# A hybrid pooling and linear-attention block in fp32: the norm row spread by a product, P4 second in the first pair, values of a head pair asked for among the gates

## The chip, the cores and the metric

One NeuronCore of a Trainium2 chip runs the whole block. The metric is the device time of one execution in microseconds (us); smaller is better. The core has a matrix engine (TensorE, PE in the profile; PEld is its loading of stationary operands), a vector engine (VectorE, DVE), a scalar engine (ScalarE, ACT), GpSimd (POOL) and SyncE (SP), which here only issues DMA transfers. Matrix products accumulate in PSUM, which the kernel uses as eight banks of 128 x 512 fp32; everything else lies in the on-chip memory or in DRAM. A bank can be written again once the engine that reads it is through.

## What is computed

The reference, cut to what matters (L is 16 meta tokens and 1024 tokens, D is 1024, the inner width of the MLP 4096, four heads of key width 64 and value width 128, chunks of 64):

```python
def rmsnorm(x, g):
    return x * lax.rsqrt(jnp.mean(x * x, axis=-1, keepdims=True) + EPS) * g

def hybrid_mixer(u, ...):
    z = jnp.einsum('bld,dn->bln', u, w_in)
    a, q, k, v, r, lr, ga, gb = jnp.split(z, IN_SPLITS, axis=-1)
    p = multiscale_pool(a)                      # trailing means over 2, 4, 8, 16 tokens, minus the token
    ...
    y_a = jnp.einsum('blc,cd->bld', p, w_pool_out)
    log_a = jax.nn.log_sigmoid(lr @ w_gate_up + b_gate) / GLA_TAU
    o = gla_chunked(q, k, v, log_a)             # chunked gated linear attention with a carried state
    o = rmsnorm(o, gla_norm) * jax.nn.silu(r)
    y_b = jnp.einsum('blc,cd->bld', o, w_gla_out)
    m = jax.nn.sigmoid(ga) * y_a + jax.nn.sigmoid(gb) * y_b
    return jnp.einsum('bld,de->ble', m, w_out)

def reference(x, meta_tokens, norm_mix, ...):
    h = jnp.concatenate([meta, x], axis=1)
    h = h + hybrid_mixer(rmsnorm(h, norm_mix[l]), ...)
    h = h + squared_relu_mlp(rmsnorm(h, norm_ffn[l]), w_ff1[l], w_ff2[l])
    return rmsnorm(h, norm_final)[:, N_META:]
```

## The kernel before

**Products.** Every large product is computed as three products of a reduced fp32 type: an operand is split into a high half (copied with rounding by ACT) and a low half (the remainder, subtracted by DVE), and `mm3` (L256) issues high by high, low by high and high by low (L260 to L262). Weights arrive from DRAM as `raw` tiles, and their split is a step on ACT (L609, L75, L341) and one on DVE (L610, L76, L342). Tile names in the profile follow this: `th` and `tl` are the halves of the activations, `w1h` and `w1l` those of a weight, `fs` and `s` sums of weight blocks that POOL or DVE make.

**Opening (`start`, L390 on).** `load(t)` brings a tile of 128 tokens of x, `layer_norm` (L227) normalizes it: ACT squares and sums, DVE makes the inverse root and multiplies by it and by `gB`, the weights of the norm repeated on all 128 partitions (L234, tile `us`). `gB` is filled by one transfer (L414). `transposed` (L238) turns a tile on PE into banks `ms` and `sc` (L246), from which ACT and DVE make `th` (L202) and `tl` (L203). `v_tile` (L350) makes the values of a tile and of the first two heads, with 16 more columns, `lr`, which DVE copies to `lrtok` (L364); the values go to DRAM as `v_dram`. `ask_vw` and `load_vw` (L331, L336) load and split the weights of the values (`vw`) and `lrraw`, those of the lr columns. `warm` (L409) multiplies a blank tile, so that PE has something to do: six products of 512 columns before the first tile, more small ones later.

**Eleven pairs of projections (`pairs_of_projections`).** Each pair of 128-column projections of q, r and the two gates, on both halves of the tokens, is computed by seven products P1 to P7 of sums of blocks instead of eight products of blocks. P1 and P2 of a pair share one bank of kind `sc`; ACT copies P1 away as `u2p` (L720) before P2 is added. P5 and P3 share a bank of kind `z`, of which there are two; P4, P6 and P7 take one of two banks `y`. DVE adds P6 to `u2p` (L724), P7 to that, giving `u3p` (L726), and then makes two of the four results: `c` from P5 and `u3p` (L728), and `c` from P4 and `u3p` (L732). `pairs_order` (L633) sets the order: P1, P2, P5 of the first pair, then seven products at a time, from pair i and the one before. `ahead(..., 3)` has the weights of each product split three products earlier; the first one's are made in `first_pair`, before the stage. Beside these products ACT, DVE and POOL work on the chunks of the attention: keys, decays, and the q values, which come back from `q_dram` as `gi` (L852) and are copied by ACT to `f` and `n` (L865).

**Attention and gates.** `gla_open` (L917) asks for the attention's inputs (`gi`), for gates (`ask`, L957: from `ga_dram`, later from `gb_dram` with the sums in `ma_dram`; 16 tiles of L965 in a ring) and for the values (`v`, L937). `across` (L1040 on) transposes the keys (L1055), copies them to `kt` (ACT, L1056), and multiplies them with the values (L1061). Where it yields a number, other products (output products of the pooling mixer and of the attention, bank `mm`) are put on PE in between, for that many us times `PACE` (L1127). A gate is opened by ACT (an exponential, L970), and the output products are read with it by DVE (L1025, L1026).

**What sets the order.** PE runs its instructions in the order in which the program is written, and so the kernel's generators (`ahead`, the yields, `pour`) decide it. For ACT, DVE, POOL and SP a scheduler orders the instructions when the program is built; each of these runs its row strictly in order. All transfers of the program go through SP's row.

**After it.** The MLP: FF1 by seven products as above (rows `b_sc`, `b_z`, `b_y` until 926 us), then FF2 (`b_o`), whose first product waits for DVE (L1361), and the last norm.

Of the kernel before, what the change touches and what calls it, by code (L numbers as in the profile page):

```python
# [11 lines left out]
ALU = mybir.AluOpType  # L12
# [18 lines left out]
MP = 264  # L31
PACE, LEVEL, OPENING, STRETCH = 1.3, 1.6, 6.0, 1.9

# [70 lines left out]
def kernel(  # L104
# [286 lines left out]
    def start():  # L391
# [19 lines left out]
        load(0)  # L411
        warm(6)
        nc.sync.dma_start(ident, ident_in)
        nc.sync.dma_start(gB, bcast(norm_mix))  # L414
# [145 lines left out]
    k_(1)  # L560
    step(one, lambda: S["last_difference"]())

# [70 lines left out]
    def pairs_order(n_pairs):  # L633
        yield from (("P1", 0), ("P2", 0), ("P5", 0))
        for i in range(1, n_pairs + 1):
            for p in ("P6", "P1", "P7", "P5", "P4", "P2", "P3"):
                n = i if p in ("P1", "P5", "P2") else i - 1
                if n < n_pairs:
                    yield p, n

    def sums_weights(order, n_pairs, load, eng):
# [5 lines left out]
        for p, i in order(n_pairs):  # L647
# [3 lines left out]
            else:  # L651
                a21, a22 = (w1raw[i, 1][:, k : k + 4] for k in (0, 4))
                s = quad(S["fs"][:, i % 2] if p != "P7" else S["s3"])
                if p == "P5":
# [33 lines left out]
    def pairs_of_projections():  # L688
# [18 lines left out]
        for n, (p, i, (ah, al)) in enumerate(ahead(pair_weights(), 3)):  # L707
# [3 lines left out]
            elif p in ("P5", "P3"):  # L711
                b = zb[i] = bank("z") if p == "P5" else zb[i]
            else:
                b = bank("y")
# [10 lines left out]
            elif p == "P7":  # L725
# [3 lines left out]
                put(d + 1, 1, c, c)  # L729
            elif p == "P4":  # L730
                c = nxt("c")
# [15 lines left out]
            if total - n <= 6:  # L747
                assert chain is None
                if total - n > 2:
                    pooled_part(n - total + 6)  # L750
            if total - n == 3:
                raw.back()
                W1.shift = 1
                enqueue(rest)
                W1.top_up(1)
            yield
# [160 lines left out]
    def gla_open():  # L917
# [11 lines left out]
        lend("c", "t1", "o")  # L929
        wanted[:] = [("a", d, h) for d in range(8) for h in range(2)] + [("b", d, 0) for d in range(8)]  # L930
        for p in range(2):
            fetch(p, 0)
        ask()
        for half in range(2):
            for p in range(2):
                t = slice(4 * half, 4 * half + 4)
                nc.sync.dma_start(S["v"][:, p, t], v_dram[p, t].rearrange("t p c -> p t c"))  # L937
        banks(keep=1, mm=3, m2=1, ms=1)
# [15 lines left out]

    def ask():

        while wanted:  # L957
            kind, d, h = wanted[0]
# [82 lines left out]
    def across(p, half):  # L1041
# [14 lines left out]
        act.activation(kt, b, ACT.Copy)  # L1056
        yield 1.4
        kv = wide2().rearrange("p u (j c) -> p u j c", j=4)
# [477 lines left out]
```

## Time and profile before

| | |
|---|---|
| three runs | 1250.29, 1251.13, 1251.39 us; median 1251.13 |
| the profiled execution, own time | 1249.28 us |
| its span | 1247.4 us |
| mean granted clock of PE | 0.996 |
| PE busy | 1213.6 us, 97% of the span |
| weight loads (PEld) | 997.3 us, 80% (beside PE) |
| DVE busy | 866.0 us, 69% |
| ACT busy | 635.3 us, 51% |
| POOL busy | 72.2 us, 6% |
| HBM | 153 GB/s over the span |

The span is the stretch between the first and the last instruction of the profiled execution; its own time is that of the whole launch. PE's row of the page is at 9 tenths or more in all but the first and the last of 40 slices, so that what is idle on PE lies in short waits. They are to be found in the list of waits, and each of them then in a window of single rows: start and length in us, engine, line, operation, written tile `<-` read tiles, shape, and in brackets the idle time before it with the tile for which the engine waited.

### The profile page before, as it was taken

What the parts mean: (1) busy time and instruction counts of PE and PEld (TensorE: products, weight loads), DVE (VectorE), ACT (ScalarE), POOL (GpSimd) and SP (SyncE); (2) the same over time, 40 slices, a digit from 0 to 9 for tenths busy, and PEclk for the clock granted to TensorE, in tenths of its full rate; (3) what the DMA queues carried; (4) which work ended last, traced back from release to release, by engine and by line L of the source; (5) the groups of instructions that cost most, each with busy time, mean ns of one, the idle gap of its engine ahead of it and who ended that gap; (6) DMA issues with size and microseconds to landing.
All of it is one profiled execution on the core that took longest, in us unless ns stands there. A gap on an engine that the chain in (4) does not pass through costs nothing.

```text
span 1247.4 us, 18416 instructions
## 1 busy us (share of the span) xinstructions
PE 1213.6 (97%) x6807; PEld 997.3 (80%) x6807; DVE 866.0 (69%) x1421; ACT 635.3 (51%) x1119; POOL 72.2 (6%) x95
## 2 busy tenths in 40 slices
PE   8999999999999999999999999999999999999997
PEld 6999877777777778788778888888878788888776
DVE  5635548796877478844897676676664887887686
ACT  7623456767576434523655454554554444445454
POOL 0000042322321000000000000000000000000000
PEclk9999999999999999999999999999999999999999
DMA  8212342434347976941245444444579763333532
GB/s 259 81 39 85 94 127 76 136 97 141 80 134 229 327 264 200 311 138 51 101 125 161 145 157 150 157 152 144 168 241 368 274 214 102 102 93 93 169 91 86
DMA packets 153401, 192.23 MB, mean 154 GB/s; under 512 B 12096, under 2 KB 89168, under 8 KB 153312
## 3 DMA queue, kind: packets, MB, share of 16 engines
q1 hardware_dynamic: 153312, 191.06, 47.6%
q8 instruction: 53, 0.87, 0.3%
q14 instruction: 36, 0.29, 0.1%
HBM read 129.14 MB, written 61.88 MB: 153 GB/s over the span
## 4 chain that ended last, share of the span: by engine, by line
PE 76%; DVE 9%; DMA 8%; ACT 4%; issue 3%; SPq 1%; POOL 0%; DVEq 0%; ACTq 0%; POOLq 0%
PE b_o L261 7%; PE b_o L262 7%; PE b_o L260 7%; PE b_mm L262 6%; PE b_mm L260 6%; PE b_mm L261 6%; PE b_y L260 5%; PE b_y L261 5%; PE b_y L262 5%; PE b_sc L260 3%; PE b_sc L261 3%; PE b_z L260 3%; PE b_sc L262 3%; PE b_z L261 3%; PE b_z L262 3%
## 5 line engine op out<-in xcount | busy, mean ns | idle before, releaser
L609 ACT ACTIVATE w1h<-raw 128x512 fp32r<-128x512 f32 x106 | 66.0, 624 | 61.0 <-PE b_sc L261 19.5
L260 PE MATMUL b_sc<-th,w1h 128*128 128x512 f32 x216 | 86.4, 400 | 2.5 <-ACT u2p L720 1.8
L261 PE MATMUL b_sc<-tl,w1h 128*128 128x512 f32 x216 | 85.5, 396 | 0.0
L260 PE MATMUL b_z<-th,w1h 128*128 128x512 f32 x216 | 85.3, 395 | 0.2 <-DVE c L728 0.2
L262 PE MATMUL b_sc<-th,w1l 128*128 128x512 f32 x216 | 85.1, 394 | 0.0
L610 DVE TENSOR_TENSOR w1l<-raw,w1h 128x512 fp32r<-128x512 f32 x106 | 72.5, 684 | 18.0 <-ACT w1h L609 18.0
L261 PE MATMUL b_z<-tl,w1h 128*128 128x512 f32 x216 | 84.2, 390 | 0.4 <-DVE tl L1221 0.4
L262 PE MATMUL b_z<-th,w1l 128*128 128x512 f32 x216 | 84.1, 390 | 0.0
L260 PE MATMUL b_o<-w1h 128*128 128x512 f32 x192 | 75.6, 394 | 2.8 <-DVE h L1361 1.8
L609 ACT ACTIVATE w1h<-fs 128x512 fp32r<-128x512 f32 x81 | 50.9, 629 | 51.7 <-PE b_y L261 29.9
L261 PE MATMUL b_o<-w1l,w1h 128*128 128x512 f32 x192 | 75.6, 393 | 1.4 <-DVE w1l L610 1.4
L262 PE MATMUL b_o<-w1h,w1l 128*128 128x512 f32 x192 | 75.5, 393 | 0.1
L260 PE MATMUL b_mm<-th,w1h 128*128 128x512 f32 (+1 forms) x208 | 72.0, 346 | 0.9 <-DVE c L736 0.9
L610 DVE TENSOR_TENSOR w1l<-fs,w1h 128x512 fp32r<-128x512 f32 x81 | 56.8, 702 | 20.7 <-ACT w1h L609 20.6
L261 PE MATMUL b_mm<-tl,w1h 128*128 128x512 f32 (+1 forms) x208 | 71.1, 342 | 0.0
L262 PE MATMUL b_mm<-th,w1l 128*128 128x512 f32 (+1 forms) x208 | 71.0, 341 | 0.0
L609 ACT ACTIVATE w1h<-bt 128x512 fp32r<-128x512 f32 x45 | 28.3, 630 | 56.8 <-issue 33.0
L1409 DVE TENSOR_TENSOR bt<-w,w 128x512 f32<-128x512 f32 x80 | 54.7, 684 | 2.7 <-DMA w<-in_w_ff_dram 2.7
L260 PEld LDWEIGHTS b_sc<-th,w1h 128*128 128x128 f32 x216 | 40.9, 190 | 13.5 <-ACT u2p L720 2.2
L261 PE MATMUL b_o<-fxl,fxh 128*128 128x512 f32 x128 | 49.9, 390 | 0.7 <-DVE small L219 0.7
L260 PE MATMUL b_mm<-wo,th 128*128 128x512 f32 x128 | 50.4, 394 | 0.0
L262 PE MATMUL b_o<-fxh,fxl 128*128 128x512 f32 x128 | 49.9, 390 | 0.0
(375 smaller groups left out, 3345.7 us busy)
## 6 DMA issues: line engine op xcount, KB each, us to landing
hf_dram<-h SPq DMA_DIRECT2D x112, 256.0 KB, 2.1
raw<-hf_dram SPq DMA_DIRECT2D x112, 256.0 KB, 2.6
w<-in_w_ff_dram SPq DMA_DIRECT2D x64, 256.0 KB, 4.7
raw<-in_w_in_dram SPq DMA_DIRECT2D x22, 512.0 KB, 4.7
raw<-in_w_ff_dram SPq DMA_DIRECT2D x16, 512.0 KB, 4.2
rawx<-in_w_ff_dram SPq DMA_DIRECT2D x16, 512.0 KB, 4.3
rawp<-in_w_in_dram SPq DMA_DIRECT2D x10, 512.0 KB, 4.6
xs<-in_x_dram SPq DMA_DIRECT2D x8, 512.0 KB, 5.5
```

Of the source, the lines that this page charges most:

```text
L260: pe.matmul(ps, ah, bh, start=first and i == 0, stop=False, skip_group_check=more)
L261: pe.matmul(ps, ah, bl, start=False, stop=False, skip_group_check=more)
L262: pe.matmul(ps, al, bh, start=False, stop=last and i == n - 1, skip_group_check=more)
L609: act.activation(hi, a, ACT.Copy)
L610: dve.tensor_tensor(lo, a, f32(hi), ALU.subtract)
L1409: dve.tensor_tensor(bt, w, S["w2"][q[3:]][:, i], ALU.add if q[2] == "+" else ALU.subtract)
```

## The change

The diff without its rows of numbers:

```diff
-PACE, LEVEL, OPENING, STRETCH = 1.3, 1.6, 6.0, 1.9
+PACE, LEVEL, OPENING, STRETCH = 1.3, 1.6, 5.0, 1.9
...
         load(0)
-        warm(6)
+        nc.sync.dma_start(um[:1], norm_mix[None, :])
         nc.sync.dma_start(ident, ident_in)
-        nc.sync.dma_start(gB, bcast(norm_mix))
+        ask_vw(0)
+        nc.sync.dma_start(S["lrraw"], w_in[:, C_LR : C_LR + 16].rearrange("(k p) c -> p k c", p=P))
+        pool.memset(xm[:1, :P], 1.0)
+        warm(2)
+        for c in halves():
+            b = bank("mm")
+            pe.matmul(b, xm[:1, :P], um[:1, c], start=True, stop=True)
+            dve.tensor_copy(gB[:, c], b)
+        warm(2)
         for t in range(8):
...
             if t == 0:
-                nc.sync.dma_start(S["lrraw"], w_in[:, C_LR : C_LR + 16].rearrange("(k p) c -> p k c", p=P))
-                ask_vw(0)
                 load(1)
...
-    step(one, lambda: S["last_difference"]())
+    def after_keys():
+        S["first"] += [next(S["pw"]) for _ in range(2)]
+        S["last_difference"]()
+
+    step(one, after_keys)
...
     def pairs_order(n_pairs):
-        yield from (("P1", 0), ("P2", 0), ("P5", 0))
+        yield from (("P1", 0), ("P4", 0), ("P2", 0), ("P5", 0))
         for i in range(1, n_pairs + 1):
             for p in ("P6", "P1", "P7", "P5", "P4", "P2", "P3"):
                 n = i if p in ("P1", "P5", "P2") else i - 1
-                if n < n_pairs:
+                if n < n_pairs and (p, n) != ("P4", 0):
                     yield p, n
...
+            elif (p, i) == ("P4", 0):
+                b = early = bank("z")
             else:
                 b = bank("y")
...
                 put(d + 1, 1, c, c)
-            elif p == "P4":
+                if i == 0:
+                    c = nxt("c")
+                    dve.tensor_tensor(c, early, u3, ALU.add)
+                    put(d + 1, 0, c, c)
+            elif p == "P4" and i:
...
+        def values(p, half):
+            t = slice(4 * half, 4 * half + 4)
+            nc.sync.dma_start(S["v"][:, p, t], v_dram[p, t].rearrange("t p c -> p t c"))
+
+        ask(2)
         for p in range(2):
             fetch(p, 0)
+            values(p, 0)
         ask()
-        for half in range(2):
-            for p in range(2):
-                t = slice(4 * half, 4 * half + 4)
-                nc.sync.dma_start(S["v"][:, p, t], v_dram[p, t].rearrange("t p c -> p t c"))
+        for p in range(2):
+            values(p, 1)
...
-    def ask():
+    def ask(most=16):
 
-        while wanted:
+        while wanted and S["io_live"] < most:
...
         act.activation(kt, b, ACT.Copy)
-        yield 1.4
+        yield 2.4
         kv = wide2().rearrange("p u (j c) -> p u j c", j=4)
```

Three lines that do nothing else are left out: the loads of W1 before the last three products stand a few lines earlier, and the sum for P4 needs no buffer of its own.

**The opening.** One row of the norm's weights (4 KB) is loaded to `um`; PE multiplies a row of ones with it, once for each half, and DVE copies the two results from PSUM to `gB` (L421 of the changed kernel). The six warming products become two ahead and two behind these. The weights of the values are asked for at the start, `lrraw` behind them.

**The first pair.** P4 is computed second, into a bank of kind `z`, and read (L744 of the changed kernel) after P7, since it needs `u3p`. On DVE's row, before, from the sum with P6 on (`rawp` and `raw` are loaded weights, L610 makes the low half of one):

```order
L724 TENSOR_TENSOR u2p<-b_y,u2p 128x512 [waits PE_49]
L610 TENSOR_TENSOR w1l<-raw_123,w1h 128x512 [waits DMAHW0_49,Activation_49]
L610 TENSOR_TENSOR w1l<-rawp_1639,w1h 128x512 [waits PE_49,Activation_49]
L726 TENSOR_TENSOR u3p<-b_y,u2p 128x512 [waits DVE_49,PE_49]
L610 TENSOR_TENSOR w1l<-fs,w1h 128x512 [waits Activation_49]
L728 TENSOR_TENSOR c<-b_z,u3p 128x512 [waits DMAHW7_49,DMAHW3_49,DVE_49]
L610 TENSOR_TENSOR w1l<-fs,w1h 128x512 [waits PE_49,Activation_49]
L732 TENSOR_TENSOR c<-b_y,u3p 128x512 [waits DMAHW4_49,DMAHW0_49,PE_49]
```

and of the change:

```order
L736 TENSOR_TENSOR u2p<-b_y,u2p 128x512 [waits PE_49]
L620 TENSOR_TENSOR w1l<-rawp_1646,w1h 128x512 [waits Activation_49]
L620 TENSOR_TENSOR w1l<-fs,w1h 128x512 [waits PE_49,Activation_49]
L738 TENSOR_TENSOR u3p<-b_y,u2p 128x512 [waits DVE_49,PE_49]
L620 TENSOR_TENSOR w1l<-fs,w1h 128x512 [waits Activation_49]
L740 TENSOR_TENSOR c<-b_z,u3p 128x512 [waits DMAHW7_49,DMAHW3_49,DVE_49]
L744 TENSOR_TENSOR c<-b_z,u3p 128x512 [waits DMAHW4_49,DMAHW0_49]
```

The reading of P4 moved up behind that of P5, from another bank. On PE's row P5 of the second pair, the first product behind P7, waits for DVE's reading at L744, since the ring of two z banks is full; before, this row waited for the high half on ACT alone. Elsewhere in the stage the rows of ACT, DVE and SP keep their order, apart from the weights of P4, P2 and P5, which are split two products earlier.

**Values among the gates.** SP's row at the opening of the attention (L584 is a store of gates, L965 or L985 the load of one, `v<-v_dram` the values of one head pair and half; four in all), before:

```order
L584 DMA ga_dram<-t_1011 128x512 [waits DMAHW4_49,DVE_49]
L965 DMA c<-ga_dram 128x512 [waits DMAHW5_49,Activation_49]
L937 DMA v<-v_dram 128x4x256 [waits DMAHW6_49,PE_49]
L584 DMA ga_dram<-t_1011 128x512 [waits DMAHW7_49,DVE_49]
L965 DMA c<-ga_dram 128x512 [waits DMAHW0_49,Activation_49]
L584 DMA ga_dram<-t_1011 128x512 [waits DMAHW1_49,DVE_49]
L965 DMA c<-ga_dram 128x512 [waits DMAHW2_49,Activation_49]
L965 DMA t_1011<-ga_dram 128x512 [waits DMAHW4_49,DMAHW3_49]
L965 DMA t_1011<-ga_dram 128x512 [waits DMAHW7_49]
L965 DMA t_1011<-ga_dram 128x512 [waits DMAHW5_49,DMAHW1_49]
L937 DMA v<-v_dram 128x4x256 [waits DMAHW6_49]
```

and of the change:

```order
L594 DMA ga_dram<-t_1014 128x512 [waits DMAHW4_49,DVE_49]
L949 DMA v<-v_dram 128x4x256 [waits DMAHW5_49,PE_49]
L594 DMA ga_dram<-t_1014 128x512 [waits DMAHW6_49,DVE_49]
L985 DMA c<-ga_dram 128x512 [waits DMAHW7_49,Activation_49]
L949 DMA v<-v_dram 128x4x256 [waits DMAHW0_49]
L594 DMA ga_dram<-t_1014 128x512 [waits DMAHW1_49,DVE_49]
L985 DMA c<-ga_dram 128x512 [waits DMAHW2_49,Activation_49]
```

The second head pair's values moved from behind seven loads of gates and the three stores among them to the place behind the second.

**Later rows that moved.** The longer yield after `kt` shifts six products of other work ahead of the state products in one half, and six in the other. Between 470 and 525 us the scheduler also places loads and splits otherwise; on SP's row, around the load of a weight of the attention's output (`in_w_gla_out`), before:

```order
L965 DMA o<-ma_dram 128x512 [waits DMAHW4_49]
L965 DMA t_4838<-gb_dram 128x512 [waits DMAHW5_49,DVE_49]
L965 DMA t_4838<-ma_dram 128x512 [waits DMAHW6_49]
L965 DMA t_4838<-gb_dram 128x512 [waits DMAHW7_49]
L965 DMA t_4838<-ma_dram 128x512 [waits DMAHW0_49]
L99 DMA raw_4852<-in_w_gla_out_dram 128x4x256 [waits DMAHW1_49]
```

and of the change:

```order
L985 DMA o<-ma_dram 128x512 [waits DMAHW3_49]
L99 DMA raw_4855<-in_w_gla_out_dram 128x4x256 [waits DMAHW4_49]
L985 DMA t_4841<-gb_dram 128x512 [waits DMAHW5_49,DVE_49]
L985 DMA t_4841<-ma_dram 128x512 [waits DMAHW6_49]
L985 DMA t_4841<-gb_dram 128x512 [waits DMAHW7_49]
L985 DMA t_4841<-ma_dram 128x512 [waits DMAHW0_49]
```

The weight load moved ahead of four loads of gates and sums, and its low half on DVE moved ahead with it. Outside these places (the opening to 30 us, 150 to 180, 404 to 525) each engine's row is the same as before.

More of the change, by code (lines that the diff above doesn't have):

```diff
@@ L652, in sums_weights @@
                 a21, a22 = (w1raw[i, 1][:, k : k + 4] for k in (0, 4))
-                s = quad(S["fs"][:, i % 2] if p != "P7" else S["s3"])
+                s = None if p == "P4" else quad(S["fs"][:, i % 2] if p != "P7" else S["s3"])
                 if p == "P5":
@@ L748, in pairs_of_projections @@
                 assert chain is None
+                if total - n == 3:
+                    raw.back()
+                    W1.shift = 1
+                    enqueue(rest)
+                    W1.top_up(1)
                 if total - n > 2:
                     pooled_part(n - total + 6)
[L751 to L755, printed above, removed]
             yield
```

## The prediction

> **What bounds the kernel now.** I read the page's head first, then the waits of the matrix engine (PE), then windows around the two longest, and only then single rows.
>
> ```profile
> span 1247.4 us, 18416 instructions
> PE 76%; DVE 9%; DMA 8%; ACT 4%; issue 3%; SPq 1%; POOL 0%; DVEq 0%; ACTq 0%; POOLq 0%
> ```
>
> The first line is the span of the profiled execution, whose own time is 1249.28 us: 1.9 us lie around the span, and it stands 1.85 us under the median of the runs, 1251.13. The second is the chain of work that ended last: three quarters of it are PE. Nothing else is a bound for long, so a change is worth what it adds to or takes from PE's idle time, and what it does to PE's clock.
>
> ```profile
> PE b_sc L260 <- ACT u2p L720: 1.8, 1, 1.8
> PE b_o L260 <- DVE h L1361: 1.8, 1, 1.8
> PE b_m L1061 <- ACT kt L1056: 1.6, 1, 1.6
> PE b_sc L1061 <- DMA v<-v_dram: 1.5, 1, 1.5
> PE b_mm L260 <- ACT th L202: 1.2, 1, 1.2
> PE b_mm L260 <- ACT w1h L75: 1.1, 1, 1.1
> PE b_sc L246 <- DVE lrtok L364: 1.0, 1, 1.0
> PE b_mm L262 <- DVE w1l L76: 0.6, 1, 0.6
> PE b_mm L260 <- DVE t L1025: 0.5, 1, 0.5
> ```
>
> These are PE's waits: who waited, for whom, us in total, times, longest. Each happens once. The change touches all but the second of them (the start of the last stage, far behind every edit).
>
> ```profile
> 154.34:157.75 3.41, 1.60 (x8) 1.00 (x7) 1.16 (x2) 1.11 (x2) 2.78 (x4) 1.00 0.70 185
> 157.75:161.16 3.41, 3.41 (x10) 2.65 (x9) 1.22 (x3) 1.15 (x2) 1.52 (x3) 0.50 0.73 195
> 925.75:929.16 3.41, 1.65 (x7) 0.94 (x7) 3.41 (x7) 1.79 (x4) 0.00 (x0) 1.00 0.92 321
> 929.16:932.57 3.41, 3.41 (x9) 2.62 (x9) 2.11 (x4) 0.44 (x1) 0.00 (x0) 0.50 0.99 324
> 452.68:456.09 3.41, 1.88 (x9) 1.18 (x7) 2.12 (x3) 1.06 (x3) 0.00 (x0) 1.00 0.71 196
> ```
>
> Windows: the stretch, its length, busy time of PE, weight load, DVE, ACT and POOL, then the granted clock. I cut them at multiples of 3.413 us from 7.56, where the clock's changes fall in this trace. Where PE was busy for 1.60 or 1.65 of 3.41 us, the next 3.41 us ran at clock 0.50; with 1.88 it stayed at 1.00. So about 1.71 us of idle inside one such window costs, besides itself, half of the next, 1.7 us. The wait for u2p therefore costs 1.81 + 1.70 = 3.5 us, and that for h as much.
>
> The Trainium skill ("TensorE: Matmul & The Clock Gate", Part 1: The HAM clock gate (the "warmup" mystery)) gives a free-running window of 4096 cycles at 1.2 GHz, 3413 ns, which this trace's changes of clock fit; it names an idle window of about 3.4 us as what halves the clock, and there the trace differs: 1.81 and 1.76 us of idle inside one window sufficed.
>
> **The opening: −1.0 us.**
>
> ```profile
> 1.45 8.44 PE L409 MATMUL b_ms<-xr 128*128 128x512 f32 x12 [1.45 <-POOL xr L405]
> 1.65 0.42 SPq L414 DMA_DIRECT2D gB<-in_norm_mix_dram  x1
> 7.06 1.28 DVE L234 SCALAR_TENSOR_TENSOR us<-xs,small,gB 128x1024 f32<-128x1024 f32 x1
> 9.73 0.60 PE L246 MATMUL b_sc<-ident,us 128*128 128x128 f32 x4
> 17.82 0.63 PE L246 MATMUL b_sc<-ident,us 128*128 128x128 f32 x4 [0.99 <-DVE lrtok L364]
> ```
>
> Removed: a 512 KB transfer. Added: two products of one row by 512, which take the place of two of the six warming ones, and two copies of 128x512 from PSUM. Six warming products are 12 records in 8.44 us: at half clock one record is about 0.85 us, at full 0.43. Two warming products end near 4.9, the two new ones near 6.6 and 8.0 (clock full from 7.56); the copies, at 0.68 each (the row of 174.79 below is a reading of PSUM of this size), end near 7.3 and 8.7; the normalized row then takes its 1.28 and ends at about 10.05 instead of 8.34. But its transposes could not begin before 9.73 anyway, behind the warming products: only 0.3 us are lost. Gained: the raw weights of the values come 512 KB sooner and ahead of the small lr block, whose split leaves the head of DVE's row, and the fifth tile of x is asked for before the first store of values, which waits for ACT on the same queue. The waits of 0.99 (lrtok) and 1.22 (th) hang on these. I take the first as gone and 0.3 of the second: 0.3 − 0.99 − 0.3 = −1.0. Bounds: −1.5 (most of both waits goes, none of it lost to the splits, which still fill DVE) and +1.5 (both stay and the 1.7 us delay of the first row comes through).
>
> **The first pair: +2.0 us.**
>
> ```profile
> 152.62 0.40 PE L260 MATMUL b_sc<-th,w1h 128*128 128x512 f32 x1
> 157.39 0.50 PE L260 MATMUL b_sc<-th,w1h 128*128 128x512 f32 x1 [1.81 <-ACT u2p L720]
> 164.58 0.39 PE L260 MATMUL b_y<-t0h,w1h 128*128 128x512 f32 x1
> 170.10 0.40 PE L260 MATMUL b_y<-t1h,w1h 128*128 128x512 f32 x1
> 168.31 0.34 SPq L852 DMA_DIRECT2D gi<-q_dram  x1
> 170.79 0.88 ACT L865 ACTIVATE f<-gi 128x512 f32<-128x512 f32 x1 [2.88 <-DMA gi<-q_dram]
> 172.33 0.62 ACT L609 ACTIVATE w1h<-rawp 128x512 fp32r<-128x512 f32 x1
> 173.59 0.68 DVE L726 TENSOR_TENSOR u3p<-b_y,u2p 128x512 f32<-128x512 f32 x1
> 174.79 0.69 DVE L728 TENSOR_TENSOR c<-b_z,u3p 128x512 f32<-128x512 f32 x1
> 178.47 0.69 DVE L732 TENSOR_TENSOR c<-b_y,u3p 128x512 f32<-128x512 f32 x1 [1.09 <-PE b_y L262]
> ```
>
> P1 begins at 152.62, P2 at 157.39 after the wait for the copy u2p (both use the same bank), P6 at 164.58, P7 at 170.10: two products apart, 5.52, so 2.76 each. With P4 between P1 and P2 the copy is covered: −1.81, and the half clock behind it goes: −1.70. P4 itself is no extra work, it came later.
>
> P4 now fills one of the two z banks, and both are full until P7 has been combined. P5 of the next pair needs one; it waits for DVE to read `early`, where before it waited for ACT alone. Seven products from 152.62 end P7 at about 172.0. DVE cannot answer at once: ahead of u3p in its row stands a low half whose high half on ACT is behind the chunk copies, and these begin at 170.79, when gi lands, whatever PE does. So DVE's chain stays where it was: u3p at 173.59, the low half after it at 174.19, c at 174.79, and, one pitch of 0.60 on, the new reading of `early` from 175.39 to 176.08. PE waits 176.08 − 172.03 = 4.05 us, where before it had two products, P5 and P4, to run. Behind it waits everything on PE; what is late next is P2 of the second pair: 176.1 + 2.76 = 178.8, against 172.85 + 2 × 2.76 = 178.4 before. In the window 171.40 to 174.81 PE would be idle 2.8 us, so the next, to 178.22, runs at half clock, and PE loses half of the 2.1 us left of it: 1.1, at another phase up to 2.4; I take 1.5. Sum: −1.81 − 1.70 + 4.05 + 1.5 = +2.0. Bounds: −3.5 + 0.6 (DVE gets at `early` as soon as P7 ends, 172.0 + 0.6) = −2.9, and +4 (DVE one low half later, and 2.4 of clock).
>
> By the Trainium skill's rule (the same section) the wait of 4 us would have to fill a window of 3.41 us whole, which at this phase it does not; the 1.5 would fall away. The rows of 154.34 and 925.75 speak against it, so it gets no chance of its own.
>
> **Values and gates of the attention: −1.5 and −1.0 us.**
>
> ```profile
> 416.63 1.53 SPq L937 DMA_DIRECT2D v<-v_dram  x3
> 420.68 1.10 PE L1061 MATMUL b_sc<-v,kt 64*64 64x128 f32 x32 [1.54 <-DMA v<-v_dram]
> 455.02 0.63 ACT L970 ACTIVATE o<-o 128x512 f32<-128x512 f32 x1 [2.77 <-DMA o<-gb_dram]
> 455.56 0.58 ACT L1056 ACTIVATE kt<-b_ms 128x512 f32<-128x512 f32 x1
> 456.19 1.10 PE L1061 MATMUL b_m<-v,kt 64*64 64x128 f32 x32 [1.64 <-ACT kt L1056]
> ```
>
> The second head pair's values are asked for at 416.63, behind seven gate loads on SP, and are used at 420.68 after 1.54 us of wait. Now they stand behind the first two gates, some 7 us sooner, while the landing took 3.9 (416.63 to about 420.5): the wait goes, −1.5 (bounds −1.54 and 0). The gates passed come some 1 to 2 us later; DVE works on them while PE transposes.
>
> The yield of 2.4 instead of 1.4, times PACE 1.3, puts 1.3 us more of other products on PE between the transposes and the state products. At 456.19 PE had waited 1.64 for kt, which stood on ACT behind a gate that waited for its transfer: 1.64 − 1.3 leaves 0.3. I take −1.0, since the second yield shifts as much work the other way; bounds −1.6 and 0.
>
> **The gated output products, 494 to 525 us: 0.**
>
> ```profile
> 505.18 0.43 SPq L99 DMA_DIRECT2D raw<-in_w_gla_out_dram  x1
> 511.42 1.04 ACT L75 ACTIVATE w1h<-raw 128x1024 fp32r<-128x1024 f32 x1
> 512.57 1.22 DVE L76 TENSOR_TENSOR w1l<-raw,w1h 128x1024 fp32r<-128x1024 f32 x1
> ```
>
> A weight load moves ahead of four loads of gates and sums, and with it its split on ACT and DVE. The waits on w1h and w1l (1.1 + 0.6) go, −1.7. But the low half, 1.22 us, now stands ahead of the reading of t that frees a bank, and the wait for that was 0.5: it becomes 1.7, +1.22. The gates behind the load on SP come 0.43 later, and the tiles they go into as much: +0.43. Sum −0.05, about 0. Bounds: −1.7 (DVE has room after all) and +4.6, which the second rival works out.
>
> **The clock at 929.**
>
> ```profile
> 928.41 0.47 PE L260 MATMUL b_o<-w1h 128*128 128x512 f32 x1 [1.76 <-DVE h L1361]
> ```
>
> The wait lies from 926.65 to 928.41, all in the window 925.75 to 929.16, and only just over 1.71. The parts sum to −1.0 + 2.0 − 1.5 − 1.0 + 0 = −1.5. Shifted so, it would begin at 925.15 and be cut by the window's edge into 0.6 and 1.16: neither halves the clock, −1.7. This holds when PE arrives there over 0.9 us sooner or over 0.75 later (then the other edge, 929.16, cuts the wait), again with every 3.41 us more, and when the windows keep their phase from the start of the span. So the forecast is −1.5 − 1.7 = −3.2: span 1244.2, own time of a profiled execution 1246.1, median 1251.13 − 3.2 = **1247.9**.
>
> **Rivals.** (1) The phase of the windows is free, or the wait falls whole into another one, and the half clock at 929 remains: −1.5, 1249.6. For it: 1.76 us fall whole into 3.41 by chance about half the time (1.65 of 3.41). Against: all changes of clock in this trace lie on one grid. (2) Slower, by one mechanism: DVE's row in the gated output products. If the load's delay adds to the low half's at the same reading of t, the wait is 0.5 + 1.22 + 0.43 = 2.1 us, over the 1.71 from which the clock halves: +1.7. Then the low half itself waits for the same late row, so that the 1.7 gained on the weights does not come: +1.7; and the next tile's reading is behind it by another 1.22. Together +4.6 on −1.5, so +3.1, 1254.2; PE comes to 929 later by 3.1, where the wait lies whole in a window again and nothing is gained. For it: DVE has hardly a gap there, and 1.7 is on the threshold. Against: the delay on SP need not meet the same reading. It decides from 1.71 us of idle. (3) The opening loses: one-row products may not count as activity, the clock comes up one window later, four records cost 0.4 us more each, and the normalized row's delay comes through: +1.5 in place of −1.0. The wait at 929 is then 1.0 later and is cut by the other edge, −1.7: −0.7 in all, 1250.4. For it: 127 of 128 rows carry nothing; against: PE's busy time counts them, and the clock followed that. (4) The pair costs less: the wait for `early` stays under 1.71 and halves no clock. That is −2.35 − 1.5 = −3.85 more, at 929 the wait is cut again: 1251.13 − 1.5 − 3.85 − 1.7 = 1244.1. For it: ACT and DVE have half their time free; against: gi lands at 170.8 whatever PE does. That P4's move merely changes one wait for another is in the forecast already.
>
> **How the numbers follow.** Forecast 0.40; (1) 0.20; (2) 0.17; (3) 0.11; (4) 0.12. With a tenth left out at each end the range goes from about (4), 1244.3, past (1) and (3) almost to (2), 1253.5; the forecast's own, from the parts' smaller errors, is 1246.2 to 1249.5. What a measurement of this kernel can tell from no change is about 0.2%, 2.5 us, so faster means under 1248.6. The forecast is 0.7 below that: of its 0.40 I give 0.29 to faster and 0.11 to the same. (4) is all faster, (1) and (3) add 0.07 of their 0.31 to faster and 0.03 to slower, the rest is the same; of (2) 0.16 is slower. Faster 0.48, same 0.33, slower 0.19.
>
> **What would show it.** Right: no wait for u2p near 157, a wait of about 4 us of PE for DVE c before a product on b_z near 172 with half clock behind it; no wait for v at 419; less than 0.6 for kt near 455; transposes at about 16.8 instead of 17.8. Wrong: the wait on b_z under 2 us or over 5; full clock reached at 11 instead of 7.6; a wait of over 1.7 for t or c near 508. My sum fails first where the parts interact: the phase of the clock's windows makes each of them worth 1.7 more or less.

## The result and the profile after

The changed kernel took 1258.15 us (median of 7 runs, 1254.60 to 1261.88) beside 1250.69 us for the kernel before (7 runs, 1246.78 to 1254.14): a ratio of 1.006 with a 95% interval of 1.0036 to 1.0085. It is slower by 7.5 us. The profiled execution took 1255.42 us, 6.1 more than that of before. The head of its page:

```profile
span 1253.4 us, 18425 instructions
PE 1211.8 (97%) x6807; PEld 995.4 (79%) x6807; DVE 867.2 (69%) x1423; ACT 635.2 (51%) x1119; POOL 73.6 (6%) x96
```

Its list of waits on PE (us in total, times, longest):

```profile
PE b_z L260 <- ACT c L584: 5.1, 1, 5.1
PE b_mm L260 <- DVE t L1045: 2.6, 1, 2.6
...
PE b_mm L260 <- DVE c L1045: 2.1, 1, 2.1
PE b_mm L260 <- ACT th L1049: 2.0, 1, 2.0
PE b_o L260 <- DVE h L1381: 1.8, 1, 1.8
PE b_m L1104 <- DVE small L1099: 1.7, 1, 1.7
...
PE b_o L260 <- ACT fxh L619: 1.2, 1, 1.2
```

PE is busy 1.8 us less than before (1213.6) and idle 7.8 us longer, and its mean granted clock is the same, 0.996: in this execution the 6 us are waits. The waits for u2p and for v are gone, and the first four rows here are new or several times longer than before (t 0.5, c 0.6). A table of stages, from the starts of PE's rows in the traces, shows where the time lies (us; e1 to e14 are experiments below):

| stage | before | changed | e1 | e2 | e5 | e9 | e10 | e14 |
|---|---|---|---|---|---|---|---|---|
| start to the first P1 | 152.6 | 150.7 | 150.9 | 155.5 | 151.0 | 150.7 | 153.6 | 151.8 |
| P1 to the first product on `b_gs` from `n` | 44.4 | 47.9 | 42.8 | 48.5 | 40.7 | 40.8 | 40.8 | 40.8 |
| to the first product of v and kt | 221.0 | 220.2 | 223.9 | 220.6 | 222.1 | 220.9 | 222.5 | 221.2 |
| to the first product with wo | 100.9 | 106.2 | 100.3 | 103.3 | 106.5 | 104.2 | 107.2 | 100.4 |
| to FF2 | 409.5 | 409.2 | 409.0 | 410.4 | 409.9 | 409.3 | 409.0 | 409.2 |
| FF2 to the end | 319.0 | 319.2 | 318.7 | 319.5 | 319.1 | 318.4 | 318.3 | 319.0 |

Against before the opening takes 1.9 us less, the first pair 3.5 more, the keys 0.8 less, and the attention with the gated output products 5.3 more.

**The first pair.** Rows of the changed kernel (start, length, engine, line, operation):

```profile
159.66 0.58 ACT L584 ACTIVATE c<-b_sc 128x512 f32<-128x512 f32 x1
161.81 0.37 SPq L99 DMA_DIRECT2D raw<-in_w_in_dram  x1
162.27 0.53 SPq L585 DMA_DIRECT2D q_dram<-c  x1
167.26 0.34 SPq L868 DMA_DIRECT2D gi<-q_dram  x1
169.76 0.86 ACT L881 ACTIVATE f<-gi 128x512 f32<-128x512 f32 x1 [4.68 <-DMA gi<-q_dram]
...
171.91 0.69 DVE L620 TENSOR_TENSOR w1l<-fs,w1h 128x512 fp32r<-128x512 f32 x1 [5.44 <-ACT w1h L619]
172.53 0.68 DVE L738 TENSOR_TENSOR u3p<-b_y,u2p 128x512 f32<-128x512 f32 x1
...
174.48 0.68 DVE L744 TENSOR_TENSOR c<-b_z,u3p 128x512 f32<-128x512 f32 x1
175.31 0.76 PE L260 MATMUL b_z<-th,w1h 128*128 128x512 f32 x1 [5.14 <-ACT c L584]
```

The wait ends with DVE's reading of P4's bank (L744, until 175.16); the profile names an ACT row that ended at about the same time. Ahead of it stands the predicted chain: gi, ACT's copies, a low half, u3p. New is its beginning: the q values are ready at 160.24 and their store is issued at 162.27, behind a weight load that SP issues at 161.81, once POOL has ended a sum of weights (`fs`, 159.52 to 161.78). In the kernel before the same two stood so:

```profile
162.33 0.58 ACT L574 ACTIVATE c<-b_sc 128x512 f32<-128x512 f32 x1
162.91 0.37 SPq L99 DMA_DIRECT2D raw<-in_w_in_dram  x1
163.37 0.53 SPq L575 DMA_DIRECT2D q_dram<-c  x1
```

There it was half a us from the end of the copy to the store, since POOL's sum (until 162.88) and the copy (until 162.91) ended together; now it is 2.0. And the clock, in windows as before (PE's busy time first, the granted clock in the third place from the right):

```profile
168.91:172.32 3.41, 1.26 (x6) 0.72 (x4) 0.41 (x1) 2.56 (x5) 0.00 (x0) 1.00 0.08 30
172.32:175.73 3.41, 0.42 (x1) 0.45 (x2) 2.84 (x5) 1.70 (x4) 3.04 (x4) 0.50 0.00 0
175.73:179.15 3.42, 3.42 (x9) 2.65 (x9) 0.00 (x0) 0.09 (x1) 0.19 (x1) 0.50 0.61 128
```

The wait spoils two windows, so the clock stays at half for 6.8 us; PE is at work in 3.8 of them and loses 1.9. (In this execution the windows begin at 5.07 plus multiples of 3.413 us; in that of before it was 7.56. This offset of the windows, their phase, is another one in each execution.)

### The profile page after: what moved, and what is told of

Its sections match the earlier page's. It is cut to its first block, busy times and chain, and to the rows that moved or that the text cites. A ratio compares the mean times of both kernels' runs of the same rounds, so it can differ in the third digit from the quotient of the medians.

```text
span 1253.4 us, 18425 instructions
## 1 busy us (share of the span) xinstructions
PE 1211.8 (97%) x6807; PEld 995.4 (79%) x6807; DVE 867.2 (69%) x1423; ACT 635.2 (51%) x1119; POOL 73.6 (6%) x96
## 4 chain that ended last, share of the span: by engine, by line
PE 64%; DVE 9%; DMA 7%; ACT 3%; issue 2%; SPq 0%; DVEq 0%; ACTq 0%
PE b_o L261 7%; PE b_o L262 7%; PE b_o L260 7%; PE b_y L260 5%; PE b_y L261 5%; PE b_y L262 5%; PE b_z L260 3%; PE b_z L261 3%; PE b_z L262 3%; PE b_mm L260 3%; PE b_mm L262 3%; PE b_mm L261 3%; PE b_sc L260 3%; PE b_sc L261 3%; PE b_sc L262 3%
## 5 line engine op out<-in xcount | busy, mean ns | idle before, releaser
L260 PEld LDWEIGHTS b_z<-th,w1h 128*128 128x128 f32 x216 | 41.0, 190 | 15.3 <-ACT c L584 5.5
```

Of the source, the lines that this page charges most:

```text
L260: pe.matmul(ps, ah, bh, start=first and i == 0, stop=False, skip_group_check=more)
```

## The experiments

All times are medians of 12 executions (7 for the changed kernel itself); the kernel before beside them, 35 executions in each set, had medians of 1251.10 (e1 to e4), 1251.17 (e5 to e8), 1251.34 (e9 to e12) and 1252.04 (e13 to e16). The ratio is not the quotient of the two medians and can differ from it by 0.1%.

| | what is in it | us | ratio to before, 95% interval |
|---|---|---|---|
| e1 | opening | 1249.90 | 0.9989 (0.9967 to 1.0011) |
| e2 | P4 second | 1256.80 | 1.0041 (1.0018 to 1.0064) |
| e3 | values among the gates | 1251.31 | 0.9991 (0.9971 to 1.0011) |
| e4 | yield 2.4, OPENING 5.0 | 1253.14 | 1.0008 (0.9989 to 1.0027) |
| e5 | all, P4 copied out of its bank | 1249.54 | 0.9988 (0.9971 to 1.0005) |
| e6 | opening, P4 copied | 1248.52 | 0.9971 (0.9953 to 0.9990) |
| e7 | e3 and e4 together | 1253.48 | 1.0017 (0.9997 to 1.0037) |
| e8 | e6 with the values | 1248.67 | 0.9983 (0.9966 to 1.0000) |
| e9 | e5 without the yield | 1248.20 | 0.9981 (0.9964 to 0.9999) |
| e10 | e5 without OPENING 5.0 | 1252.49 | 1.0002 (0.9985 to 1.0020) |
| e11 | e5, low halves of wo on POOL | 1253.22 | 1.0005 (0.9991 to 1.0018) |
| e12 | e6, low halves of wo on POOL | 1249.41 | 0.9988 (0.9971 to 1.0004) |
| e13 | e1, norm row by products of 128 rows | 1248.60 | 0.9980 (0.9961 to 0.9999) |
| e14 | e6, norm row by products of 128 rows | 1247.66 | 0.9966 (0.9949 to 0.9982) |
| e15 | e9, norm row by products of 128 rows | 1251.54 | 0.9997 (0.9980 to 1.0014) |
| e16 | e5, two more tiles for gates | 1252.06 | 1.0002 (0.9984 to 1.0019) |

The executions of one kernel differ by up to 12 us. In the 35 of before beside e1 the time goes with the time lost to half clock (the span times one less the mean clock): the correlation is 0.82, the slope 0.93, and the loss 6.3 us in the mean. Differences of a us between two medians decide nothing here; what follows rests on the traces, of which there is one for each kernel.

**The four edits alone (e1 to e4).** Each is the hunks of the diff that belong to it. The rows of the opening and of the pair are moved by their own edits alone, and the values move rows of SP and ACT only between 404 and 420 us.

> The opening alone on the kernel before. Theory 1 (each edit has its own account: opening -1.8, pair +3.5, values -1.5, yields +5): 1.8 us faster than before, third tile's first product at about 23.8 instead of 25.7, no wait on lrtok. Rival (the opening's gain in the changed kernel is the phase of the clock's windows, which there gave full clock at 5.07 instead of 7.56): the gain moves with the time of full clock, half a us for each us, and is about 0.6 where the clock comes at 7.5.

> P4 second in the first pair alone. Theory 1: no wait on u2p, a wait of 4 to 5 us on b_z near 172 to 176 that ends with DVE's reading of P4's bank, half clock for one or two windows behind it; 2 to 3.5 us slower than before. Rival (the opening's lead made this wait, since gi lands whatever PE does): the wait is 4.0 here and not 5.1, and the loss under 2.

> The values asked for among the gates alone; yield and OPENING as before. Theory 1: the wait of 1.54 on v near 420 goes, nothing else moves, 1.5 us faster. Rival (the gates that the values passed come late, and this causes the long waits between 480 and 525): waits of 2 us and more for t, c and th at 497, 514 and 525, 3 us slower.

> The yield of 2.4 and OPENING of 5.0 alone. Theory 1: the shifted filler products reorder DVE's, ACT's and SP's rows between 470 and 525, the waits there grow from 2.8 to about 7.5 us in sum, 4 to 5 us slower; the wait on kt shrinks by 0.5. Rival (the values' edit did it): within 1 us of before.

The opening gains about a us, which its interval does not tell from none. P4 second loses 5.7 by itself, more than the 2 to 3.5 expected; its trace has 4.2 us more than before in the pair's stage, and a wait for v of 3.8 where before had 1.5. Waits on PE in e2 and then in e3:

```profile
PE b_z L260 <- ACT c L578: 5.3, 1, 5.3
PE b_sc L1071 <- DMA v<-v_dram: 3.8, 1, 3.8
```

```profile
PE b_m L1065 <- ACT kt L1060: 2.2, 1, 2.2
...
PE b_m L1088 <- DVE small L1083: 1.7, 1, 1.7
```

In e2 PE came to the pair 4.9 us later than in the changed kernel (first P1 at 155.5, 150.7), and the wait on b_z is the same: the chain through gi comes later with PE, so the rival that the opening's lead made this wait falls. In e3 the wait for v is gone as expected, but a new one of 1.7 on DVE's `small` stands in its place, and that on kt has grown from 1.6 to 2.2; no gain is left. The other traces repeat this. In the ten with the values' edit nothing waits for v, and PE waits 1.05 to 3.0 us for `small` near 432; in the eight without it PE waits 1.5 to 3.8 us for v and under 0.4 for `small`. The long waits after 490 do not come with the values, so that rival falls too. With the yield (e4) they come in part: 2.7 us on t near 513. The median is 2.0 us above before, which the interval does not tell from none; 4 to 5 had been expected.

**Is it the bank (e5, e6)?** P4 keeps its bank, but is copied away at once:

```diff
             elif (p, i) == ("P4", 0):
-                b = early = bank("z")
+                b = bank("z")
...
+            elif p == "P4" and i == 0:
+                early = S["u3p"][:, 1]
+                act.activation(early, b, ACT.Copy)
```

> The changed kernel, but ACT copies P4 of the first pair out of its bank at once, and DVE adds the copy later, so that the bank is free long before P5 of the second pair. Theory 1 (the wait of 5.1 us on b_z is the bank that P4 holds until P7 is combined): the wait goes whole, with the half clock behind it; 5 to 7 us faster than the changed kernel. Rival (P5 would wait anyway, for its weights or for ACT's row behind the copies of gi): a wait of 2 us or more stays at the same product.

> The opening and P4 second with the copy, without the edits of the attention. Theory 1 (opening and the covered u2p wait are gains, each for itself): about 1.2 for the opening and 1.8 to 3.5 for u2p, 3 to 4.5 us faster than before. Rival (the gains are taken back at the next fixed arrival, gi or v): the wait on v near 420 grows by what was gained, within 1 us of before.

The wait on b_z is gone in e5 (P5 of the second pair begins at 170.32, right behind P7), the stage falls from 47.9 to 40.7 us, and the median is 8.6 us below that of the changed kernel (5 to 7 had been expected). So the bank that waited to be read was the cause; the copy costs one ACT row for which PE does not wait. Against 42.8 in e1, where P2 waits 1.8 for u2p at full clock, P4 second with the copy gains 2.1 in this stage, and 3.6 against the execution of before in which that wait also halved the clock. e6 is faster than both kernels, by 2.6 us against before, a little less than the 3 to 4.5 expected; the wait for v did not grow (1.6), so its rival falls.

**Values and yields (e7 to e10).** e7 is e3 and e4 together, e8 is e6 with the values; e9 and e10 are e5 with one number back:

```diff
-        yield 2.4
+        yield 1.4
...
-PACE, LEVEL, OPENING, STRETCH = 1.3, 1.6, 5.0, 1.9
+PACE, LEVEL, OPENING, STRETCH = 1.3, 1.6, 6.0, 1.9
```

> Values among the gates, yield 2.4 and OPENING 5.0 together, opening and pair as before. Theory 1 (they interact: without the wait on v, PE comes to the gated output products earlier and finds DVE's row fuller): waits of 7 us in sum between 490 and 526, 3 to 5 us slower than before, more than the sum of the two apart (-0.6 and +1.4 in the means). Rival (the long waits there in the changed kernel belong to that one execution): at most 2 us slower.

> The opening, P4 second with the copy, and the values among the gates; yield and OPENING as before. If the values' edit gains nothing by itself, since the waits on DVE at 434 and on kt at 457 take the place of that on v: the same as the run without it, 3 to 4.5 us faster than before. If it gains its 1.5: 4.5 to 6 us faster.

> As the changed kernel with P4's copy (e5), but the yield back at 1.4; values and OPENING 5.0 stay. If the longer yield takes the filler that the gated output products lack later: the waits on t and c between 490 and 515 fall from 4.5 to under 2.5 us in sum, a wait on kt of 1.5 to 2.5 comes back near 453; about 1 us faster than e5. If OPENING does it: the same as e5 within 1 us, long waits stay.

> As e5, but OPENING back at 6.0; values and yield 2.4 stay. Other half of the same question: if the yield does it, long waits on t and c stay (4 us or more in sum) and the time is that of e5 within 1 us; if OPENING does it, they fall under 2.5 and it is 1 to 2 us faster.

e8 is where e6 is: the values give nothing here either. Of the two numbers it is the yield that makes the wait on t. Waits of e5, e9 and e10:

```profile
PE b_mm L260 <- DVE t L1048: 2.5, 1, 2.5
...
PE b_mm L260 <- DVE c L1048: 2.1, 1, 2.1
```

```profile
PE b_sc L1107 <- DVE small L1102: 3.0, 1, 3.0
```

```profile
PE b_mm L260 <- DVE t L1048: 3.9, 2, 3.3
PE b_mm L260 <- DVE o L1019: 2.0, 1, 2.0
PE b_mm L262 <- DVE w1l L76: 2.0, 2, 1.8
```

Without the yield (e9) the waits on c and t fall to nothing and 0.6. With it and without OPENING 5.0 (e10) that on t grows to 3.3, the one on c is gone, and others of 2.0 on o and 1.8 on a weight's low half are there. Over all traces the wait on t is the steady one: its longest is 2.2 to 3.3 us in the seven with the longer yield and 0.4 to 1.1 in the eleven without. The others change from trace to trace: a wait on c of 2 us stands in the changed kernel, e5 and e11 alone, one of 2.0 on th, at the first product with wo, in the changed kernel alone, and no run shows what makes them. The yield does what it was meant for: the wait on kt is under 0.4 in six of the seven and 1.1 in the changed kernel, and up to 2.5 without it. The stage from the first product of v and kt to wo takes 104.0 to 107.2 us in the seven traces (mean 105.8), and 100.3 to 104.2 in the eleven (mean 102.3): 3.4 us, half clock included. In the medians e10 lies 3.0 above e5, where within 1 was expected; the spread of the executions is too wide to read more from that. e7's loss of 2.3, not told from none, is under what was expected and near the sum of its parts: the two edits do not add much to each other.

**What holds PE there (e11, e12, e16).** In e11 and e12 one word is changed, in e16 one number:

```diff
-            dve.tensor_tensor(wo[:, 1], r, f32(wo[:, 0]), ALU.subtract)
+            pool.tensor_tensor(wo[:, 1], r, f32(wo[:, 0]), ALU.subtract)
...
-        buffer("t1", 4)
+        buffer("t1", 6)
```

> As e5, but the low halves of the eight blocks of the output weight (wo, 1.2 us each on DVE) are made by POOL, which is idle there. Theory (PE's waits on t, c and th between 490 and 526 are DVE's full row): DVE reads the banks earlier, the waits fall by 1 to 3 us in sum, 1 to 3 us faster than e5. Rival (gates and weights land late, DVE waits too): the waits stay within 0.5 us.

> The same move of wo to POOL on the opening and P4's copy alone (e6). If DVE's row is what is left there: the waits of 1.2 and 1.3 near 493 and 512 shrink, up to 1.5 us faster than e6. If POOL's work slows DVE or comes late for the first product with wo: equal or slower.

> As e5 (the changed kernel with P4's copy), with two more tiles in the ring of gates of the second half, so that four gates more can be under way. Theory (the wait of 2.5 near 510 is a gate that lands late, since its load waits for a tile that DVE frees): that wait falls under 1.2, the one of 2.0 on c near 492, which is DVE's full row in the first half, stays; 1 to 1.5 faster than e5. Rival (DVE's row is what is late there too): both waits stay within 0.5.

Eight blocks less on DVE changed neither wait (2.0 and 2.5 in e11), so wo's low halves are not what is late; the medians are 3.7 and 0.9 above those of e5 and e6, and in e12 PE now waits 0.8 for a low half of wo from POOL. Two more tiles left the wait on t at 2.2 and shortened that on c from 2.1 to 1.3, which the theory had not said. But the load of the gate in question goes out in e16, too, only when DVE ends the reading of the tile before (501.49, right behind 501.46), so the run does not show what a gate that is asked for sooner would give. The rows of the changed kernel around the wait on t that ends at 514.51:

```profile
505.30 0.44 SPq L99 DMA_DIRECT2D raw<-in_w_gla_out_dram  x1
508.11 0.32 SPq L985 DMA_DIRECT2D t<-gb_dram  x1
```

```profile
511.53 1.06 ACT L75 ACTIVATE w1h<-raw 128x1024 fp32r<-128x1024 f32 x1 [1.14 <-DMA raw<-in_w_gla_out_dram]
512.50 0.61 ACT L990 ACTIVATE t<-t 128x512 f32<-128x512 f32 x1
```

```profile
512.62 1.23 DVE L76 TENSOR_TENSOR w1l<-raw,w1h 128x1024 fp32r<-128x1024 f32 x1 [1.50 <-ACT w1h L75]
513.77 0.68 DVE L1045 TENSOR_TENSOR t<-b_mm,t 128x512 f32<-128x512 f32 x1
```

The weight is asked for at 505.30 and split from 511.53; DVE stands idle for 1.5 us, makes the low half, and only then reads t and frees the bank. The gate for t is ready at 513.11 itself, so the low half delays the reading by some 0.7, and the gate by the rest. The gate is late from its load on, which is issued at 508.11, when DVE has ended the reading of the tile before (508.08), and lands at 512.11; in the kernel before the same load was issued at 503.38 and landed at 506.62, 1.3 us before PE came to the product; now PE is there at 511.92, before it lands. That is read from the rows; no run separates the low half from the gate, and it stays open which of them a better order should mend.

Whether such a wait also halves the clock is the phase's doing. Windows of the changed kernel and of e5 around the waits on t:

```profile
510.24:513.65 3.41, 1.68 (x8) 1.06 (x6) 1.72 (x2) 2.27 (x4) 0.00 (x0) 1.00 1.00 352
513.65:517.06 3.41, 2.55 (x11) 2.10 (x12) 3.41 (x6) 1.88 (x4) 0.00 (x0) 1.00 0.82 285
```

```profile
506.79:510.21 3.42, 0.93 (x5) 0.47 (x4) 2.29 (x3) 3.04 (x4) 0.00 (x0) 1.00 0.87 337
510.21:513.62 3.41, 3.41 (x10) 2.64 (x9) 3.41 (x6) 2.10 (x3) 0.00 (x0) 0.50 0.70 216
```

In the first an edge cuts the 2.6 us and the clock stays; in the second 2.5 us fall whole into a window and the next runs at half.

The phase also decides about half clocks where PE hardly waits. In 14 windows, near 238 us in seven traces and near 297 in seven, PE was busy for 2.3 to 2.8 us, and yet the next window ran at half. The first of e6, and two groups of PE's rows in it:

```profile
238.65:242.06 3.41, 2.79 (x12) 1.49 (x12) 2.14 (x5) 2.28 (x4) 1.00 (x2) 1.00 0.45 151
242.06:245.47 3.41, 3.41 (x10) 2.66 (x9) 0.69 (x1) 2.10 (x5) 0.43 (x1) 0.50 0.19 73
```

```profile
238.79 0.43 PE L834 MATMUL b_gs<-gB 16*64 16x128 f32 x4
239.84 1.12 PE L798 MATMUL b_gs<-gB,wgu 16*128 16x512 f32 x2 [0.62 <-DVE S L838]
```

These are products of 16 rows: they use 16 of PE's 128 rows. Without them PE was busy for 0.9 to 1.4 us in each of the 14 windows. In the profiled executions of before and of the changed kernel the edges cut these places (1.5 and 1.7 us left in one window) and the clock stayed. e1 takes 2.8 us more than before in the stage of the keys; its trace has both windows, and each costs up to 1.7.

**The opening's late clock (e13 to e15).** In three of the ten traces with the new opening and products of one row (e6, e10, e11) the clock came up at 13.2 to 13.9 us instead of 4.3 to 5.1, and the first P1 began at 153.3 to 153.6 instead of 150.7 to 151.5. The five with the old opening had full clock at 4.5 to 7.6. To see whether that is the row products' doing, they are made of 128 rows:

```diff
-        nc.sync.dma_start(um[:1], norm_mix[None, :])
+        dve.memset(us[:, 2], 0.0)
...
+        nc.sync.dma_start(us[:1, 2], norm_mix[None, :])
...
-        pool.memset(xm[:1, :P], 1.0)
+        pool.memset(us[:, 1, :P], 1.0)
...
-            pe.matmul(b, xm[:1, :P], um[:1, c], start=True, stop=True)
+            pe.matmul(b, us[:, 1, :P], us[:, 2, c], start=True, stop=True)
```

> The opening alone, but the norm row is repeated by products of 128 rows (ones times a tile that is zero but for its first row) instead of products of one row. Theory (products of one row do not count for the clock: in three of nine executions with them it came at 13.2 to 13.9 instead of 4.3 to 5.1, and the first pair began at 153.4 instead of 150.8): full clock never after 7.8, first pair at 150.5 to 152, about 0.9 faster in the mean than the opening with one row. Rival (the late clock is the phase of its windows alone): full clock at 13 comes here too in a third of the executions, no difference in the mean.

> The same products of 128 rows with P4's copy (beside e6). Theory: full clock never after 7.8, about 0.9 faster than e6 in the mean, 3.5 faster than before. Rival: as e6.

> The same products with P4's copy, the values among the gates and OPENING 5.0 (beside e9). Theory: full clock never after 7.8, about 0.9 faster than e9 in the mean. Rival: as e9.

PE's first rows in e6 and in e14, two executions of nearly one phase (window edges at 3.13 and 6.54 in e6, at 2.90 and 6.32 in e14):

```profile
5.17 3.78 PE L420 MATMUL b_mm<-um,xm 1*128 1x512 f32 x4
8.87 3.78 PE L409 MATMUL b_ms<-xr 128*128 128x512 f32 x4
12.45 0.85 PE L246 MATMUL b_sc<-ident,us 128*128 128x128 f32 x3
```

```profile
5.03 2.53 PE L421 MATMUL b_mm<-us 128*128 128x512 f32 x4
7.39 1.88 PE L409 MATMUL b_ms<-xr 128*128 128x512 f32 x4
9.66 0.66 PE L246 MATMUL b_sc<-ident,us 128*128 128x128 f32 x4 [0.39 <-DVE us L234]
```

PE is busy through the window in both. With products of one row the eight records to 12.4 stay at half clock and the transposes begin at 12.45; with 128 rows the clock is full at 6.32 and they begin at 9.66. All three traces with 128 rows had full clock at 5.0 to 6.3, but only e14 has a phase at which the clock came late with one row: the first edges lie at 2.0 and 1.6 us in e13 and e15, and with one row and an edge at 1.7 (the changed kernel) it came early too. So the cause is shown by the pair e6 and e14, and the windows with products of 16 rows bear it out. e14 is the best version found by its median, 4.4 us faster than the before of its set; the intervals do not tell it from e6. Against their own befores e13 gains 3.4 us where e1 gained 1.2, and e14 4.4 where e6 gained 2.6, as expected, though within the intervals; e15 gains 0.5 where e9 gained 3.1, against the expectation. Its trace has waits of 0.8 and 0.9 us at 20 and 21 us, on halves of the activations, a window of half clock behind them (22.1 to 25.5), and the first P1 only at 153.9. Nor did P1 begin sooner in the mean: at 151.4, 151.8 and 153.9 with 128 rows, and at 151.6 in the mean of the ten with one row. So the early clock with 128 rows is shown, and a gain in time from it is not.

## Why the prediction was wrong

The forecast was 3.2 us faster; the medians say 7.5 slower, the profiled executions 6.1. Three steps failed: the price of the wait at the first pair, the gain on the values, and above all the sum of about 0 for the gated output products.

**The opening, −1.0.** Right in kind, −1.9 in this profile, and about −1.2 in the medians of e1, which its interval does not tell from none, for the reasons given (no wait on lrtok; the normalized row starts behind the copies). The third rival's mechanism was there too, in 3 traces of 10: products of one row do not bring the clock up.

**The first pair, +2.0.** The mechanism and the place were right; the size was too small, and three of the four numbers in −1.81 − 1.70 + 4.05 + 1.5 were off. The wait was 5.1 (5.3 in e2): "DVE's chain stays where it was", with gi landing "whatever PE does", was false. The chain moves with PE, and gi's load begins 0.9 later from P1 than before, because the store of q is now issued 2 us after its values are ready, behind a weight load on SP that waits for POOL; I had read SP's queue as unchanged. The half clock cost 1.9. And the 1.70 that u2p's half clock gives back was one execution's: with the same wait of 1.8, e1, e3 and e7 lost nothing to it (42.8 us in the stage, 44.4 in before and e4). Measured: +3.5 in the stage in the changed kernel and +4.2 in e2, against before with that half clock, and +5.7 in e2's medians as a whole. The fourth rival, that the wait costs less, fell; the copy shows what a wait that goes whole would have been worth.

**Values, −1.5.** The wait for v went, the gain did not come: a wait on DVE's `small`, 1.7 us in e3 as in the changed kernel, took its place at once. I had asked what the gates that the values pass would lose, and not what PE would meet if it came sooner.

**The yield, −1.0, and the gated output products, 0.** This step failed most: with the values, the stage was to take 2.5 us less, and it took 5.3 more. The wait on kt shrank by 0.5 instead of 1.0. "It becomes 1.7" and "sum −0.05, about 0" set a gain on the weights against a longer bank wait. The gain came, the two waits of 1.1 and 0.6 on w1h and w1l went, and the bank wait on t became 2.6, not 1.7; with it came two waits that I had not listed, 2.1 on c and 2.0 on th. The second rival named the place (DVE's row, the weight's low half ahead of the reading of t) and a sum of +3.1; it had the sign. What it had wrong was the price's origin: not the clock in this execution, whose windows cut all three waits, but the number of waits, and on t a gate that is late by itself. That the yield is behind the wait on t, the seven traces with it and the eleven without show; what made those on c and th stays open.

**The clock at 929.** In the changed kernel the wait of 1.8 for h was cut by an edge and cost no clock, as forecast; FF2 took no less time: a wait of 1.2 for fxh now came, which none of the six traces with half clock there has (the slower clock covers it, by my reading; no run tests that). And the phase that I used is not a property of the kernel. In ten traces this wait of 1.76 to 1.9 had at least 1.76 us in one window: it halved the clock in six of them and not in four. So the bound of 1.71 us of idle time is not a sharp one, and what I took for −1.7 is a matter of chance.

The sum was wrong in sign because the waits of the gated output products were counted as one, because the pair's chain was priced at its old place, and because one execution's clock was taken for the kernel's.

## What to carry to other kernels

A product that is computed early to cover a wait holds its bank until it is read; if what it must be added to comes late, copy it out with an engine that has time, and the cover is free. Before a filler (other work put on PE to cover a wait) is moved to close a short wait, look at who will lack it later, and count the waits of the last stage that used it, not only the one in view. With waits near half a window of the clock, one execution's profile gives the waits, but not the time: take the difference of kernels from many executions, and the reasons from stages.

## What the runs showed of the hardware

The windows of the clock have no fixed phase to the kernel's start: the first edges lay at 0.7 (before), 1.7 (changed) or 3.1 us (e6). Products of few rows keep PE busy in its rows and count for the clock little or not at all: those of one row in e6 against e14, those of 16 rows in the 14 windows near 238 and 297 us. With both left out, the 18 traces agree on the fall: behind a window of 3.41 us at full clock with up to 1.39 us of PE busy the next always ran at half, from 1.44 to 1.75 us it went either way (1.44 in e5 and 1.63 in e3 kept it, 1.49 in e8 and 1.75 in e15 did not), and above 1.75 us it never fell. The profile models the ends of PE's rows, so its busy time is not exact. For the clock to rise a window must be nearly full: with 2.70 us of 3.41 busy (before, from the start at 1.45) or 2.77 (e2) it did not rise, with 2.84 (e8) it did.

The Trainium skill ("TensorE: Matmul & The Clock Gate", Part 1: The HAM clock gate (the "warmup" mystery)) says that the window is free-running and that the number of cold products varies from run to run, which the traces bear out (full clock at 4.3 to 13.9 us). It speaks of an idle window of about 3.4 us for the fall, where here half an idle window was enough.
